# Seven of eleven gate and up chunk pairs of each feed-forward block computed with Strassen's seven half products

## The chip, the cores and the metric

The kernel runs on one core of a Trainium2 chip. The metric is the device time of one execution in microseconds (us). Five engines of the core take part: TensorE (PE: matrix products and transposes; its weight loads are listed as PEld), VectorE (DVE), ScalarE (ACT), GpSimd (POOL) and SyncE (SP), of which the last two here do little but issue DMA transfers. Each engine takes its instructions in the order of its own list, and waits where an operand or a buffer isn't ready.

## The reference

Two transformer blocks run one after the other over 256 tokens of width 2048, in float32. The first has differential attention beside a gated recurrence (hgrn2), cross attention to a memory of 256 tokens, and a feed-forward block. The second has a pooling mixer beside gated linear attention, and a feed-forward block. Both feed-forward blocks compute the same thing, and this is what the change touches:

```python
h = rms_norm(x, ffn_pre_g)                       # 256 x 2048
gate, up = jnp.split(h @ w_ffn_in, 2, axis=-1)   # each 256 x 5632
x = x + rms_norm((jax.nn.silu(gate) * up) @ w_ffn_out, ffn_post_g)
# second block: w_ffn_gate, w_ffn_up, w_ffn_down with the same shapes
```

## The kernel before

The 256 tokens are two tiles t of 128 rows. The activations of a tile stand in SBUF, the chip's working memory, in units of 128 x 512. A weight matrix is read in column chunks of 512; the hidden width of 5632 is eleven such chunks.

**Split weights.** `wsub` (L366 to L377) fetches a slab, 256 rows of a weight matrix by 512 columns, as one tile `raw` of 128x2x512 (written 128x1024 in the profile) by a 512 KB DMA that SP issues. ACT casts it to the matmul type fp32r (`wh`, L375), and DVE subtracts the cast from the raw slab (`wl`, L376). A float32 product is then made of three matmuls: high activation by high weight, high by low, low by high. There are `RAW_BUFS` = 4 buffers for raw slabs and `SPLIT_BUFS` = 8 pairs for `wh` and `wl`. Each slab therefore gives 2 (halves) x 2 (tiles) x 3 = 12 matmuls of 128x128 by 128x512.

**Activations** are transposed on PE (`transpose4`, L304) into PSUM, the memory of eight banks in which matmuls leave their results, and split in the same way into `hi` (ACT) and `lo` (DVE), L312 and L313. `normed` transposes x times the gain without the factor of the norm; the factor `rstd` is applied later, where a result is read from PSUM.

**Groups.** `group` runs the matmuls of one column chunk for both tiles (`mm_both`, L407), and hands each tile's PSUM bank to a consumer function. Small pieces of work that follow (transposes, norms) are generators; `spawn` puts one on a list and `tick` advances all of them once after each slab's matmuls. Instructions are written in program order, and a scheduler places them on the engines by priority: what stands under `ahead()` or `high_priority(offset)` is treated as if it had been written that much earlier, so that slabs are fetched and split before they are needed, as far as the buffers go.

**A feed-forward block** (`ffn`, L886) goes through the eleven chunks in three runs of 4, 4 and 3. In each run every chunk has a gate group and an up group, so 16 slabs and 192 matmuls; the gate's PSUM goes through Silu on ACT (L903, with scale `rstd`), and DVE multiplies it with the up result and `rstd` (`hh`, L908). The product is transposed and split. After a run come four groups of the down projection over its chunks. The sum y of the runs stays in SBUF: the first run writes y (L924), the second adds to it by a DMA that POOL issues (`y<-yp`, L929), the third adds on DVE (L931). The residual x stays in SBUF too.

**The boundary** ahead of a feed-forward block: the block before ends with a norm and the residual sum (`mg`, L490, four units to a tile), and `normed` takes each unit as it comes: transposes, `hi`, `lo`, and beside them the squares (`junk`, L299) and the factor (`v`, `y`, `t`, `r`, L286 to L295).

## Time and profile before

| what | value |
|---|---|
| median of 3 runs | 2867.75 us (2863.87 to 2867.84) |
| the profiled execution: its own time, its span | 2868.39 us, 2866.6 us |
| PE busy | 2837.1 us, 99% of the span |
| DVE busy | 1609.2 us, 56% |
| ACT busy | 1420.6 us, 50% |
| mean granted clock of TensorE | 0.998 of full speed |

The span is what the trace covers; 1.8 us of the execution's own time lie outside it. Matmuls overlap, so the mean duration of one in a table is longer than what it adds; what it adds is read from the chain that ended last, or from the distance between two starts. The same holds for DVE and ACT, where the next instruction can start shortly before the one ahead of it has ended. The profile's line numbers are those of the code above.

### The profile page before, as it was taken

To read this page: it belongs to the slowest core of one execution; us is meant where nothing else is said; L and a number is where in the kernel's file an instruction comes from. 1 tells how busy PE (TensorE), PEld (TensorE's weight loads), DVE (VectorE), ACT (ScalarE), POOL (GpSimd) and SP (SyncE) were. 2 spreads that over 40 slices of the span, in tenths; PEclk is the share of its full clock that TensorE was granted. 3 is DMA by queue.
4 is the path that set the end of the run, shared out by engine and by line. 5 is a ranking of instruction groups with operands and counts; after the bars stand their busy time and mean duration, and the time that the engine had idled before them with its cause. 6 is when DMAs were issued, how large, how long until landed. Compare 5 with 4: busy or idle time off the path is not lost.

```text
span 2866.6 us, 35074 instructions
## 1 busy us (share of the span) xinstructions
PE 2837.1 (99%) x13196; PEld 2351.5 (82%) x13196; DVE 1609.2 (56%) x2131; ACT 1420.6 (50%) x2116; POOL 58.8 (2%) x105
## 2 busy tenths in 40 slices
PE   8999999999999999999999999999999999999998
PEld 6788888778888888888888898888888888888887
DVE  6666586665444454456665566555565444554455
ACT  6554575664444444445655475444464444444443
POOL 1000000000000000000000000000000000000000
PEclk9999999999999999999999999999999999999999
DMA  7555546537656667765655557666747666667763
GB/s 238 163 176 168 180 156 203 169 124 215 192 190 195 187 190 214 201 201 186 201 154 166 159 152 215 196 194 191 230 138 230 189 191 194 187 191 214 202 202 124
DMA packets 277227, 535.14 MB, mean 187 GB/s; under 512 B 17769, under 2 KB 29669, under 8 KB 277056
## 3 DMA queue, kind: packets, MB, share of 16 engines
q1 hardware_dynamic: 269040, 512.70, 58.7%
q0 software_dynamic: 7440, 19.15, 2.7%
q8 instruction: 103, 1.69, 0.2%
q10 hardware_dynamic: 576, 1.05, 0.1%
q14 instruction: 68, 0.56, 0.1%
HBM read 522.86 MB, written 5.77 MB: 184 GB/s over the span
## 4 chain that ended last, share of the span: by engine, by line
PE 93%; ACT 3%; DMA 2%; DVE 2%; issue 1%; SPq 0%; DVEq 0%; ACTq 0%
PE mm L407 83%; PE tp L304 2%; PE lps L516 2%; PE mm L422 1%; PE mm L424 1%; PE mm L423 1%; DVE wl L376 1%; ACT hi L322 1%; ACT junk L299 1%; ACT wh L375 1%; DMA raw<-w_in 1%; PE po L581 0%; PE sc L686 0%; DMA raw<-w_ffn_gate 0%; DMA x<-x 0%
## 5 line engine op out<-in xcount | busy, mean ns | idle before, releaser
L376 DVE TENSOR_TENSOR wl<-raw,wh 128x1024 fp32r<-128x1024 f32 (+1 forms) x968 | 1175.6, 1215 | 1090.4 <-ACT wh L375 1088.2
L375 ACT CAST wh<-raw 128x1024 fp32r<-128x1024 f32 (+1 forms) x968 | 1011.9, 1047 | 1169.0 <-PE mm L407 1061.5
L407 PE MATMUL mm<-wh,hi 128*128 128x512 f32 (+1 forms) x3504 | 1091.9, 392 | 0.0
L407 PE MATMUL mm<-wl,hi 128*128 128x512 f32 (+1 forms) x3504 | 1079.8, 389 | 0.0
L407 PE MATMUL mm<-wh,lo 128*128 128x512 f32 (+1 forms) x3504 | 1077.8, 388 | 0.0
L407 PEld LDWEIGHTS mm<-wh,lo 128*128 128x128 f32 x3504 | 657.0, 188 | 133.7 <-issue 0.2
L407 PEld LDWEIGHTS mm<-wl,hi 128*128 128x128 f32 x3504 | 656.5, 188 | 132.2 <-issue 0.5
L407 PEld LDWEIGHTS mm<-wh,hi 128*128 128x128 f32 x3504 | 648.7, 188 | 130.0 <-issue 5.8
L422 PE MATMUL mm<-wh,hi 128*128 128x512 f32 (+1 forms) x304 | 121.0, 398 | 2.0 <-ACT hi L322 1.5
L423 PE MATMUL mm<-wl,hi 128*128 128x512 f32 (+1 forms) x304 | 119.7, 394 | 0.3 <-DVE wl L376 0.2
L424 PE MATMUL mm<-wh,lo 128*128 128x512 f32 (+1 forms) x304 | 119.9, 394 | 0.0
L322 ACT ACTIVATE hi<-tp,vec 128x128 fp32r<-128x128 f32 x224 | 71.7, 381 | 12.2 <-DVE lo L323 8.2
L323 DVE SCALAR_TENSOR_TENSOR lo<-tp,vec,hi 128x128 fp32r<-128x128 f32 x224 | 68.3, 344 | 14.7 <-ACT hi L322 14.2
L422 PEld LDWEIGHTS mm<-wh,hi 128*128 128x128 f32 x304 | 57.6, 190 | 17.3 <-ACT hi L322 7.3
L424 PEld LDWEIGHTS mm<-wh,lo 128*128 128x128 f32 x304 | 57.5, 189 | 13.0 <-DVE lo L323 2.3
L423 PEld LDWEIGHTS mm<-wl,hi 128*128 128x128 f32 x304 | 57.7, 190 | 11.2 <-DVE wl L376 1.5
L516 PEld LDWEIGHTS lps<-qd,kd 128*128 128x128 f32 x448 | 58.3, 191 | 4.2 <-issue 0.3
L516 PE MATMUL lps<-qd,kd 128*128 128x64 f32 x448 | 56.2, 268 | 0.0
L333 ACT ACTIVATE tok<-mm,r 128x512 f32<-128x512 f32 x44 | 30.1, 690 | 33.6 <-PE mm L407 33.6
L903 ACT ACTIVATE sg<-mm,r 128x512 f32<-128x512 f32 x44 | 30.4, 690 | 28.8 <-PE mm L407 28.8
L312 ACT CAST hi<-tp 128x512 fp32r<-128x512 f32 x54 | 29.7, 589 | 20.5 <-PE tp L304 20.3
L929 POOL DMA_DIRECT2D y<-yp x16 | 13.9, 872 | 1214.1 <-ACT yp L928 1214.1
(243 smaller groups left out, 1220.1 us busy)
## 6 DMA issues: line engine op xcount, KB each, us to landing
raw<-w_in SPq DMA_DIRECT2D x256, 512.0 KB, 3.7
raw<-w_ffn_in SPq DMA_DIRECT2D x176, 512.0 KB, 3.8
raw<-w_ffn_out SPq DMA_DIRECT2D x88, 512.0 KB, 3.6
raw<-w_ffn_gate SPq DMA_DIRECT2D x88, 512.0 KB, 4.1
raw<-w_ffn_up SPq DMA_DIRECT2D x88, 512.0 KB, 3.9
raw<-w_ffn_down SPq DMA_DIRECT2D x88, 512.0 KB, 4.3
raw<-w_out SPq DMA_DIRECT2D x64, 512.0 KB, 4.3
raw<-w_branch_b SPq DMA_DIRECT2D x32, 512.0 KB, 3.7
```

The costliest lines, as they stand in the source:

```text
L304: self.nc.tensor.transpose(ps[:, i, :], src[:, i * P:(i + 1) * P], self.ident)
L322: nc.scalar.activation(hi[:, i, :], ps[:, i, :], AF.Copy, scale=g)
L323: nc.vector.scalar_tensor_tensor(lo[:, i, :], ps[:, i, :], g, hi[:, i, :].bitcast(F32), ALU.mult, ALU.subtract)
L333: self.nc.scalar.activation(dst, ps, AF.Copy, scale=scale)
L375: nc.scalar.copy(hi[:, :, :ncol], raw[:, :, :ncol])
L376: nc.vector.tensor_tensor(lo[:, :, :ncol], raw[:, :, :ncol], hi[:, :, :ncol].bitcast(F32), ALU.subtract)
L407: nc.tensor.matmul(ps[t][:, :ncol], hT[t][kk // 4][p][:, kk % 4, :], w[:, i, :ncol], start=kk == first and p == 0 and w is wh, stop=kk == ...
L422: nc.tensor.matmul(ps[:, :ncol], xh, wh[:, i, :ncol], start=kk == first, stop=False)
L423: nc.tensor.matmul(ps[:, :ncol], xh, wl[:, i, :ncol], start=False, stop=False)
L424: nc.tensor.matmul(ps[:, :ncol], xl, wh[:, i, :ncol], start=False, stop=kk == last)
L516: nc.tensor.matmul(ps[:, h, :], lhs[:, i, :], rhs[:, i, :], start=c == 0, stop=c == cph - 1)
L903: nc.scalar.activation(u, ps, AF.Silu, scale=rstd[t])
```

## The change

It concerns the gate and up products alone. With A the 256 x 2048 activations as a 2 x 2 grid (tile t by half of the 2048) and B the 2 x 2 grid of a weight column pair (half of the 2048 by gate or up), the four blocks of A @ B are eight half products. In seven of the eleven chunk pairs (1, 2, 4, 5, 7, 8, 10) the function `seven` computes them as seven products of sums, by Strassen's scheme in Winograd's form, instead. The other four pairs (0, 3, 6, 9) run as before (`plain`).

- `seven` has four steps s. A step fetches four slabs (upper and lower half of the rows, of gate and of up), forms four sums of slabs in place on DVE (L490, L493, L495, L500), and splits seven weight parts (cast L386, subtraction L387), named P1, Q3, Q5, Q7, P2, Q6, Q4. Each part has 6 matmuls (L506 to L508, 2 halves x 3), 42 to a step and 168 to a chunk pair, into seven PSUM banks. At the end one ACT copy (L512) and seven DVE sums (L513 to L519) make the four blocks; then Silu and a multiplication for each tile.
- `combos` makes the sums of activations once for each feed-forward block: 24 DVE operations and 8 ACT casts of 128x512, as a job that begins behind chunk 0.
- The activations must now be scaled ahead of the sums. `normed(scaled=True)` computes the four squares and the factor first, then makes four scaled copies (ACT), and transposes these.
- x goes to DRAM ahead of the block (`spilled`), and the partial y stays in DRAM; both are read again in the last run of down groups, x by SP and y by POOL. The chunks, fast ones marked by True, and the down runs are ordered by `FF_ORDER`, with four down runs in place of three.
- `ACT_UNITS` goes from 54 to 51 and `RAW_BUFS` from 4 to 6, in the whole program.

```diff
-ACT_UNITS = 54
-RAW_BUFS = 4
+ACT_UNITS = 51
+RAW_BUFS = 6
 SPLIT_BUFS = 8
...
+SLAB_AHEAD = 70
+POST_AHEAD = 150
+
+FF_ORDER = ((0, False), (1, True), (0, 2), (2, True), (3, False), (4, True), (2, 5),
+            (5, True), (6, False), (7, True), (5, 8), (8, True), (9, False), (10, True), (8, 11))
...
+    def combos(self, hT):
...
+        a = {(t, k): [hT[t][2 * k + j] for j in range(2)] for t in range(NT) for k in range(2)}
+        S = {"P1": a[0, 0], "P2": a[0, 1], "Q4": a[1, 1], "Q5": [None] * 2, "Q6": [None] * 2, "Q7": [None] * 2, "Q3": [None] * 2}
+
+        def split(v):
+            hi, lo = self.uT("sh"), self.uT("sl")
+            nc.scalar.copy(hi, v)
+            nc.vector.tensor_tensor(lo, v, hi.bitcast(F32), ALU.subtract)
+            return hi, lo
...
+        def job():
+            for j in range(2):
+                v21, v22 = full(1, 0, j), full(1, 1, j)
+                yield 2
+                nc.vector.tensor_tensor(v22, v21, v22, ALU.subtract)
+                S["Q5"][j] = split(v22)
+                yield 2
...
+    def seven(self, Wa, Wb, c0, S, consume):
...
+        for s in range(4):
+            with self.tc.high_priority(offset=max(0, min(SLAB_AHEAD, self.tc.cur_priority - self.base))):
+                w = {}
+                x = self.slab(Wa, 2 * s, c0)
+                w["P1"] = self.parts(x)
+                b12 = self.slab(Wb, 2 * s, c0)
+                nc.vector.tensor_tensor(x, x, b12, ALU.add)
+                b22 = self.slab(Wb, 8 + 2 * s, c0)
+                w["Q3"] = self.parts(b22)
+                nc.vector.tensor_tensor(b12, b12, b22, ALU.add)
+                w["Q5"] = self.parts(x)
+                nc.vector.tensor_tensor(x, x, b22, ALU.add)
+                w["Q7"] = self.parts(b12)
+                b21 = self.slab(Wa, 8 + 2 * s, c0)
+                w["P2"] = self.parts(b21)
+                w["Q6"] = self.parts(x)
+                nc.vector.tensor_tensor(x, x, b21, ALU.add)
+                w["Q4"] = self.parts(x)
+            for n, (wh, wl) in w.items():
+                for i in range(2):
+                    kk = 2 * s + i
+                    xh, xl = (v[:, kk % 4, :] for v in S[n][kk // 4])
+                    nc.tensor.matmul(bank[n], xh, wh[:, i, :], start=kk == 0, stop=False)
+                    nc.tensor.matmul(bank[n], xh, wl[:, i, :], start=False, stop=False)
+                    nc.tensor.matmul(bank[n], xl, wh[:, i, :], start=False, stop=kk == 7)
+                self.tick()
+        with self.tc.high_priority(offset=POST_AHEAD):
+            p1, c11, e, c12 = (self.unit(name=n) for n in ("p1", "c11", "e", "c12"))
+            nc.scalar.copy(p1, bank["P1"])
+            nc.vector.tensor_tensor(c11, bank["P2"], p1, ALU.add)
+            nc.vector.tensor_tensor(p1, bank["Q6"], p1, ALU.subtract)
...
+            if scaled:
+                acc, xs = self.small(4, "acc"), []
+                for j, u in enumerate(start(t)):
+                    self.square_sum(u, acc[:, j:j + 1])
+                    xs.append(u)
...
+                r = self.rsqrt_mean(s, D)
+                for j in range(4):
+                    u = self.unit(name="xn")
+                    self.scaled_copy(u, xs[j], r)
+                    xs[j] = u
...
-                        u = self.unit(name="hh")
-                        nc.vector.scalar_tensor_tensor(u, ps, rstd[t], sg[t], ALU.mult, ALU.mult)
...
+            for a, b in FF_ORDER:
+                if b is True:
+                    fast(a)
+                elif b is False:
+                    plain(a)
+                    if S is None:
+                        S, more = self.combos(hT)
+                        self.spawn(more)
+                else:
+                    down(a, b)
```

How the instructions stand on the engines, in three places. A row gives the line, the operation, and output <- inputs by the program's names with their numbers.

On DVE before, in the first feed-forward block where one chunk pair of a run follows another, the list is one subtraction for each slab, with the two `hh` and the two `lo` of the chunk pair in between:

```order
L376 TENSOR_TENSOR wl_1429_6630<-raw_1427_6627,wh_1428_6629 128x1024
L376 TENSOR_TENSOR wl_1432_6636<-raw_1430_6633,wh_1431_6635 128x1024
L908 SCALAR_TENSOR_TENSOR hh_1410_6593<-mm_1408_6495,r_1203_5548,sg_1382_6443 128x512
L908 SCALAR_TENSOR_TENSOR hh_1411_6595<-mm_1409_6496,r_1256_5750,sg_1383_6445 128x512
L376 TENSOR_TENSOR wl_1435_6642<-raw_1433_6639,wh_1434_6641 128x1024
L313 TENSOR_TENSOR lo_1441_6670<-tp_1438_6653,hi_1440_6669 128x512
L313 TENSOR_TENSOR lo_1443_6674<-tp_1439_6658,hi_1442_6673 128x512
L376 TENSOR_TENSOR wl_1448_6768<-raw_1446_6765,wh_1447_6767 128x1024
```

Each of these `wl` has 12 matmuls to serve.

On DVE after, the third step of chunk 2 (which follows a down run); `raw_1530`, `raw_1533`, `raw_1534` and `raw_1541` are its four slabs:

```order
L387 TENSOR_TENSOR wl_1532_6931<-raw_1530_6928,wh_1531_6930 128x1024
L387 TENSOR_TENSOR wl_1536_6940<-raw_1534_6937,wh_1535_6939 128x1024
L490 TENSOR_TENSOR raw_1530_6928<-raw_1530_6928,raw_1533_6934 128x1024
L493 TENSOR_TENSOR raw_1533_6934<-raw_1533_6934,raw_1534_6937 128x1024
L387 TENSOR_TENSOR wl_1538_6945<-raw_1530_6928,wh_1537_6944 128x1024
L387 TENSOR_TENSOR wl_1540_6950<-raw_1533_6934,wh_1539_6949 128x1024
L495 TENSOR_TENSOR raw_1530_6928<-raw_1530_6928,raw_1534_6937 128x1024
L387 TENSOR_TENSOR wl_1543_6956<-raw_1541_6953,wh_1542_6955 128x1024
L387 TENSOR_TENSOR wl_1545_6960<-raw_1530_6928,wh_1544_6959 128x1024
L500 TENSOR_TENSOR raw_1530_6928<-raw_1530_6928,raw_1541_6953 128x1024
L387 TENSOR_TENSOR wl_1547_6965<-raw_1530_6928,wh_1546_6964 128x1024
```

Seven subtractions and four sums of the same size now serve 42 matmuls. The sum L493 stands right behind L490, whose result the next `wl` needs; L500 and the last `wl` (Q4's) stand next to each other, and between them ACT has to cast the sum that L500 has just written.

At the end of the same chunk's fourth step two of the seven sums over PSUM (`c11`, `p1`) stand between those two:

```order
L387 TENSOR_TENSOR wl_1563_7042<-raw_1548_7010,wh_1562_7041 128x1024
L500 TENSOR_TENSOR raw_1548_7010<-raw_1548_7010,raw_1559_7035 128x1024
L513 TENSOR_TENSOR c11_1567_7093<-mm7_1491_6761,p1_1566_7092 128x512
L514 TENSOR_TENSOR p1_1566_7092<-mm7_1492_6762,p1_1566_7092 128x512
L387 TENSOR_TENSOR wl_1565_7047<-raw_1548_7010,wh_1564_7046 128x1024
L515 TENSOR_TENSOR e_1568_7094<-mm_1489_6759,p1_1566_7092 128x512
L387 TENSOR_TENSOR wl_1572_7111<-raw_1570_7108,wh_1571_7110 128x1024
```

The last subtraction of the chunk, `wl_1565`, comes behind them, and the sums go on between the splits of the next chunk.

On PE before, each weight slab meets both tiles (`hi_1187`, `hi_1244`):

```order
L407 MATMUL mm_1672_7881<-wh_1655_7847,hi_1187_5471 128x512
L407 MATMUL mm_1673_7882<-wh_1655_7847,hi_1244_5681 128x512
L407 MATMUL mm_1672_7881<-wl_1656_7848,hi_1187_5471 128x512
L407 MATMUL mm_1673_7882<-wl_1656_7848,hi_1244_5681 128x512
L407 MATMUL mm_1672_7881<-wh_1655_7847,lo_1188_5472 128x512
L407 MATMUL mm_1673_7882<-wh_1655_7847,lo_1245_5682 128x512
```

On PE after, one part, Q3 of chunk 2's first step, meets one sum of activations (`sh_1320` and `sl_1321`, from `combos`):

```order
L506 MATMUL mm_1488_6758<-wh_1499_6775,sh_1320_6036 128x512
L507 MATMUL mm_1488_6758<-wl_1500_6776,sh_1320_6036 128x512
L508 MATMUL mm_1488_6758<-wh_1499_6775,sl_1321_6037 128x512
L506 MATMUL mm_1488_6758<-wh_1499_6775,sh_1320_6036 128x512
L507 MATMUL mm_1488_6758<-wl_1500_6776,sh_1320_6036 128x512
L508 MATMUL mm_1488_6758<-wh_1499_6775,sl_1321_6037 128x512
```

PE's list goes from 12013 rows to 11677: 336 fewer, 24 for each of the 14 fast chunk pairs.

## Rows read from the trace of the kernel before

**Rows 1.** The page, part 1: busy time, share, instructions of each engine.

```profile
PE 2837.1 (99%) x13196; PEld 2351.5 (82%) x13196; DVE 1609.2 (56%) x2131; ACT 1420.6 (50%) x2116; POOL 58.8 (2%) x105
```

**Rows 2.** Windows over most of each feed-forward block: stretch, length, busy (instructions), clock, DMA.

```profile
640.00:1330.00 690.00, 690.00 (x3089) 571.84 (x3088) 344.30 (x308) 303.30 (x322) 9.19 (x12) 1.00 0.66 199
2172.00:2820.00 648.00, 647.90 (x2902) 536.89 (x2901) 318.16 (x284) 281.85 (x298) 9.15 (x12) 1.00 0.67 196
```

**Rows 3.** The chain that ended last, from 664 us: start, length, what.

```profile
664.07 43.57 PE mm L407 x192
707.64 0.87 PE tp L304 x8
708.52 43.54 PE mm L407 x192
```

**Rows 4.** Groups by form on DVE and ACT: busy us, mean ns, idle before.

```profile
L376 DVE TENSOR_TENSOR wl<-raw,wh 128x1024 fp32r<-128x1024 f32 x928 | 1134.9, 1224 | 1061.7 <-ACT wh L375 1059.5
...
L535 DVE TENSOR_TENSOR e<-b 128x512 f32<-128x512 f32 x56 | 38.2, 682 | 0.0
L313 DVE TENSOR_TENSOR lo<-tp,hi 128x512 fp32r<-128x512 f32 x54 | 34.8, 685 | 2.8 <-ACT hi L312 0.7
...
L908 DVE SCALAR_TENSOR_TENSOR hh<-mm,r,sg 128x512 f32<-128x512 f32 x44 | 31.0, 746 | 3.7 <-PE mm L407 3.7
...
L375 ACT CAST wh<-raw 128x1024 fp32r<-128x1024 f32 x928 | 976.7, 1054 | 1145.1 <-PE mm L407 1044.8 <-issue 45.4 <-DMA raw<-w_in 10.9
...
L928 ACT COPY yp<-mm 128x512 f32<-128x512 f32 x16 | 9.4, 587 | 11.5 <-PE mm L407 11.5
```

**Rows 5.** DVE's timeline, four pieces: start, length, instruction, idle before it.

```profile
2146.91 4.63 DVE L376 TENSOR_TENSOR wl<-raw,wh 128x1024 fp32r<-128x1024 f32 x4 [0.33 <-ACT wh L375]
...
2174.98 1.28 DVE L313 TENSOR_TENSOR lo<-tp,hi 128x512 fp32r<-128x512 f32 x2
2177.14 1.23 DVE L376 TENSOR_TENSOR wl<-raw,wh 128x1024 fp32r<-128x1024 f32 x1 [0.89 <-ACT wh L375]
2179.87 1.23 DVE L376 TENSOR_TENSOR wl<-raw,wh 128x1024 fp32r<-128x1024 f32 x1 [1.50 <-ACT wh L375]
```

**Rows 6.** The timeline of ACT and DVE: a cast and the split behind it.

```profile
2101.57 1.04 ACT L375 CAST wh<-raw 128x1024 fp32r<-128x1024 f32 x1
...
2102.64 1.23 DVE L376 TENSOR_TENSOR wl<-raw,wh 128x1024 fp32r<-128x1024 f32 x1 [0.25 <-ACT wh L375]
```

**Rows 7.** DVE's timeline at the boundary ahead of the first feed-forward block.

```profile
622.69 0.15 DVE L487 TENSOR_REDUCE pssq<-acc 128x1 f32<-128x4 f32 x1
...
623.73 0.16 DVE L292 TENSOR_TENSOR t<-t,v 128x1 f32<-128x1 f32 x1
623.92 0.15 DVE L293 TENSOR_SCALAR t<-t 128x1 f32<-128x1 f32 x1
...
624.31 2.74 DVE L490 SCALAR_TENSOR_TENSOR mg<-mg,r,mg 128x512 f32<-128x512 f32 x4
```

**Rows 8.** ACT's timeline at the same boundary.

```profile
625.09 0.63 ACT L299 ACTIVATE junk<-mg 128x512 f32<-128x512 f32 x1 [1.59 <-DVE mg L490]
...
631.10 1.28 ACT L903 ACT_TABLE_LOAD   x1
...
633.87 1.28 ACT L289 ACT_TABLE_LOAD   x1
```

**Rows 9.** PE's timeline at the start of the program.

```profile
25.34 1.08 PE L304 MATMUL tp<-ident,x 128*128 128x128 f32 x4 [3.08 <-DMA x<-x]
```

**Rows 10.** Windows at the start and at the boundary, columns as in rows 2.

```profile
20.00:25.30 5.30, 2.27 (x10) 1.36 (x8) 3.93 (x9) 3.23 (x7) 0.19 (x1) 1.00 0.92 281
25.34:29.20 3.86, 3.86 (x16) 3.38 (x17) 2.46 (x7) 3.61 (x10) 3.69 (x8) 0.56 1.01 371
592.00:642.00 50.00, 48.35 (x222) 38.15 (x221) 35.84 (x84) 37.23 (x90) 0.00 (x0) 1.00 0.33 103
```

**Rows 11.** The page, part 6: a slab's DMA, KB, us from issue to landing.

```profile
raw<-w_ffn_gate SPq DMA_DIRECT2D x88, 512.0 KB, 4.1
```

More of the change, by code (lines that the diff above doesn't have):

```diff
@@ L438, in load_x, with normed @@
         return xs
-    def normed(self, start, pre):
+    def normed(self, start, pre, scaled=False):
         rstd, hT = [None] * NT, [[None] * 4 for _ in range(NT)]
@@ L456, in job @@
                 yield 1
+            if scaled:
+                rstd[t] = r
+                return
             acc = self.small(4, "acc")
@@ L491, in add_normed, with spilled, f, boundary @@
             yield mg[j]
-    def boundary(self, start, pre):
+    def spilled(self, done, xd):
+        def f(t):
+            for j, u in enumerate(done(t)):
+                self.nc.gpsimd.dma_start(xd[t * P:(t + 1) * P, j * CW:(j + 1) * CW], u)
+                yield u
+        return f
+    def boundary(self, start, pre, scaled=False):
         xs = [None] * NT
@@ L501, in first @@
                 yield u
-        rstd, hT, job = self.normed(first, pre)
+        rstd, hT, job = self.normed(first, pre, scaled)
         return xs, rstd, hT, job
@@ L894, in run @@
         def run(job):
-            for bi, (b0, nb) in enumerate(blocks):
-                hid = [[None] * nb for _ in range(NT)]
-                last = bi == len(blocks) - 1
-                for c in range(nb):
-                    sg = [None] * NT
-                    def g_in(t, ps):
-                        u = self.unit(name="sg")
-                        nc.scalar.activation(u, ps, AF.Silu, scale=rstd[t])
-                        sg[t] = u
-                    def u_in(t, ps, c=c, sg=sg):
-                        u = self.unit(name="hh")
-                        nc.vector.scalar_tensor_tensor(u, ps, rstd[t], sg[t], ALU.mult, ALU.mult)
-                        def put(pair):
-                            hid[t][c] = pair
-                        yield from self.to_T(u, put)
-                    self.group(Wg, (b0 + c) * CW, hT, ks, g_in, apart=bi == 0 and c == 0)
-                    self.group(Wu, (b0 + c) * CW, hT, ks, u_in)
+            hid, S = [[None] * n_all for _ in range(NT)], None
@@ new lines, in put, with f, plain, g_in @@
+            def put(t, c):
+                def f(pair):
+                    hid[t][c] = pair
+                return f
+            def plain(c):
+                sg = [None] * NT
+                def g_in(t, ps):
+                    sg[t] = self.unit(name="sg")
+                    nc.scalar.activation(sg[t], ps, AF.Silu)
+                def u_in(t, ps):
+                    u = self.unit(name="hh")
+                    nc.vector.tensor_tensor(u, ps, sg[t], ALU.mult)
+                    yield from self.to_T(u, put(t, c))
+                self.group(Wg, c * CW, hT, ks, g_in, apart=c == 0)
+                self.group(Wu, c * CW, hT, ks, u_in)
@@ new lines, in fast, with all_in @@
+            def fast(c):
+                def all_in(*cs):
+                    with self.tc.high_priority(offset=POST_AHEAD):
+                        for t in range(NT):
+                            g, u = cs[2 * t:2 * t + 2]
+                            nc.scalar.activation(g, g, AF.Silu)
+                            nc.vector.tensor_tensor(u, u, g, ALU.mult)
+                    for t in range(NT):
+                        self.spawn(self.to_T(cs[2 * t + 1], put(t, c)))
+                self.seven(Wg, Wu, c * CW, S, all_in)
@@ L915, in run, with down @@
+            def down(b0, b1):
+                last = b1 == n_all
                 if last:
                     self.ln_exp_set()
+                    for t in range(NT):
+                        for n in range(4):
+                            y[t][n] = self.unit(name="y")
+                            nc.gpsimd.dma_start(y[t][n], yd[t][n])
+                    for t, row in enumerate(self.load_x(xd)):
+                        x[t][:] = row
                 for n in range(4):
```

96 lines of the change are left out of this document (64 added, 32 removed).

## The prediction

> **What bounds the kernel now.** I read the page's part 1 first: PE is busy for 99% of the span and DVE for 56% [rows 1]. Then the windows over the two feed-forward blocks, because an average says nothing of one stage: in 690 us and in 648 us PE has no idle time to speak of, at the full granted clock, while DVE works about half of each, 344.3 and 318.2 us [rows 2]. Then the chain of waits from 664 us: 192 matmuls in 43.57 us, so 0.2269 us for one, 0.87 us of transposes, and 44.45 us from one chunk pair to the next [rows 3]. So these stages are bound by PE; fewer matmuls make them shorter for as long as every other engine keeps up.
>
> The engine to ask about is DVE. A weight subtraction of 128x1024 lasts 1.224 us [rows 4], but four back to back take 4.63 us: (4.63 - 1.22) / 3 = 1.14 us from start to start. In a chunk pair they start 2.73 us apart and wait for the cast [rows 5], which itself had waited for PE to free a buffer [rows 4]. So DVE uses 1.14 of every 2.73 us there.
>
> **The matmuls.** 24 fewer in each of 14 fast chunk pairs are 336 x 0.2269 = 76.2 us, if PE stays the bound: 2868.4 - 76.2 = 2792 us, counted as all sums here from the profiled execution's own 2868.39 us, which lies 0.6 us over the median.
>
> **One step of a fast chunk.** PE needs 42 x 0.2269 = 9.53 us. DVE has seven subtractions and four sums, all of 128x1024. The sum of slabs has no row. The nearest is L535, which takes two float32 operands from SBUF and writes float32: 682 ns for 512 elements, where the subtraction of 512 takes 685 [rows 4] and starts 0.60 us after the one before [rows 5]. So I price a sum like a subtraction: 11 x 1.14 = 12.54 us. On top of that come waits inside the step. L490's result goes through L493 to the next `wl`, and a sum right behind its input starts 0.04 us after that has ended (small dependent operations: 623.73 + 0.16 to 623.92) [rows 7], not 0.08 us before: 0.1 us at each of two places. The long wait is behind L500: its result has to be written (1.22), cast on ACT (1.05) [rows 4], and the split starts 0.03 us behind the cast (2101.57 + 1.04 to 2102.64) [rows 6]. The split thus starts 1.22 + 0.04 + 1.05 + 0.03 = 2.34 us after L500, instead of 1.14: 1.2 us. Everything behind it on DVE, the next step's splits, waits too. A step is 12.54 + 0.2 + 1.2 = 13.9 us on DVE against 9.53 on PE: inside a fast chunk DVE is the bound.
>
> **How much of that is hidden.** DVE can run ahead only as far as there are `wh`/`wl` pairs: eight. When the work before a fast chunk ends, seven hold the parts of its step 0, and the eighth still holds the last slab of that work. So step 0 is hidden (13.9 us, out of 16 x 1.59 us of free DVE in a plain chunk pair), and the other three are not. From the end T of the work before: the eighth pair comes free, and behind a down run ACT first copies `yp` (0.59) [rows 4] and then casts (1.05): T + 1.6. Steps 1 and 2: 27.8. Step 3 up to L500: nine operations and its two small waits, 10.5; L500 1.14; the two sums over PSUM that stand there, 2 x 0.62, which cover the cast; the last split 1.22; the last five matmuls, which wait for it, 1.13: 15.2. Together 44.6 us, then 0.2 to the next group and 0.88 of transposes of its own: 45.7 against 44.45, +1.25. Behind a plain pair there is no `yp` (-0.35), the two `lo` of that pair are done inside the fast chunk (+1.2), and its transposes fall into PE's waits (-0.88): the same to 0.1. So 24 matmuls, 5.4 us, are saved, and nothing is left: 14 x 1.25 = +18 us. The slabs' DMAs are no part of this: a slab lands in 4.1 us [rows 11], and 16 slabs in 45.7 us are the rate of before (share 0.66) [rows 2].
>
> **Activation sums.** 24 operations of 128x512 fall on DVE in the first fast chunk, where DVE is the bound: 24 x 0.60 [rows 5] = 14.4, plus about 1 for waits on their own casts, less one 1.2 us wait behind L500 that they fill: +14.3 in each block, +29.
>
> **The boundaries.** Before, the transposes of a tile could start with its first residual unit. Now all four (2.74 from the start of the first, 0.7 of it needed before too) [rows 7], the last square (0.63) [rows 8], the factor (622.69 to 624.31, 1.6) [rows 7] and a scaled copy (no row; the ACT copy of `yp`, 0.59 [rows 4]) come first: 2.0 + 0.6 + 1.6 + 0.6 + 0.2 of hand-overs = 5.0. Two table loads of 1.28 us on ACT between factor and Silu [rows 8] have no reason left. PE hardly idles there now, 1.65 of 50 us [rows 10]: other work covers a part of the wait and may cover more or less of the longer one, so 0 to 10 each; I take 5: +10.
>
> **The start.** PE waits 3.08 us for the second tile of x [rows 9], whose transfers stand on SP behind seven slabs that need raw buffers; with six of these they go out earlier. But the DMA engines are already at a share of 0.92 there [rows 10]: 0 to -5, I take -3.
>
> **At nothing:** spills and reloads of x and y. POOL and SP issue them, partial y has a whole run of chunks to land in, and the reloads stand before the last down groups. If that cover is gone, it is a few us at the end of each block.
>
> Sum: 18 + 29 + 10 - 3 = +54: 2868.4 + 54 = 2922 us, 1.9% slower.
>
> **Bounds.** From below: no waits inside a step (12.54; a fast chunk 45.7 - 2 x 1.4 - 0.2 = 42.7, -1.75 x 14 = -25), sums of activations partly in idle time (+20), boundaries 0, start -5: 2858. From above: each operation on DVE starts only 0.03 us after the one before has ended (1.25; a step 11 x 1.25 + 1.1 = 14.9, a fast chunk about 48.8, +4.35 x 14 = +61), activation sums 24 x 0.75 (+36), boundaries +20, start 0: 2985.
>
> **Rivals.**
> (a) Faster. The mechanism is the step's time on DVE: at break-even 14d = -(29 + 10 - 3), d = -2.6, so a fast chunk takes 41.9 and, with three steps of it in sight, a step about 12.6 with the wait behind L500 still in it: the point is 1.2 us less in each step. If a sum of slabs cost half (0.57), a step were 4 x 0.57 = 2.3 shorter, a fast chunk 6.8, and the total 2922 - 14 x 6.8 = 2827. For it: no row shows a sum of this size. Against it: L535, and the eight pairs. Chance 0.11 of faster, 0.06 of landing within 0.2% of before.
> (b) The dearer step. If operations start only when the one before has ended (1.22), a step takes 14.6, a fast chunk 2.3 more, and the activation sums 2 more for each block: 2922 + 32 + 4 = 2958. Against it: 4.63 us for four [rows 5]; for it: in a fast chunk most have a dependent one close behind. Chance 0.15. The Trainium skill, "VectorE: DVE Perf Modes", section "The DRAIN you can't avoid", says that the next operation doesn't start until the pipeline is empty. By that rule 2958 would be the forecast; the four subtractions at 1.14 us that last 1.22 disagree with it by 0.08 us each, and the trace decides.
> (c) The clock. In the row before PE's wait of 3.08 us PE was busy for 2.27 of 5.30 us at a granted clock of 1.00, behind it the clock was 0.56 for 3.86 us [rows 9, 10]. In a fast step PE is busy for 9.5 of 13.9 us, with its longest wait between Q3 and Q5, about 2.0 us. If the clock stayed at its lower level, 1.2 GHz, a step would be 42 x 0.4538 = 19.1 us on PE, above DVE's 13.9, and a fast chunk 4 x 19.1 + 1.8 = 78 us, 32 longer: 2922 + 14 x 32 = 3370. Chance 0.04. The Trainium skill, "TensorE: Matmul & The Clock Gate", section "A second HAM failure mode: psum-queue depth-cycling", tells of a kernel whose short idle times between groups of matmuls made the clock go back and forth. By that rule some part of these 450 us would be lost; of the rows here only a wait of 3.08 us was followed by a lower clock.
> (d) PE stays the bound and the whole 76 us come: 2792. DVE's 11 operations against 9.53 us exclude it unless both prices are far off: 0.02, inside the 0.11.
>
> **How the numbers follow.** The forecast (2880 to 2945) has 0.64, (b) and what lies above it up to 2990 0.15, (c) 0.04, within 0.2% 0.06, faster 0.11. The measurement can't tell less than about 0.2%, 5.7 us, from no change. Slower is 0.64 + 0.15 + 0.04 = 0.83. The range goes from 2860, which takes in the no-change case and a little of (a), to 2990.
>
> **What would show it.** PE's matmuls fall by 336, DVE's busy time rises by 168 + 224 operations of 1.22 and 98 + 48 of 0.69 to about 2190 us. The chain in a fast chunk goes through `wl` and the sums on DVE, with PE waiting 6 to 7 us in it; fast chunks take 45 to 46 us, the first of each block about 60; Q4's split waits for its cast 1.2 us in three steps of four. The boundaries show squares, factor and scaled copies in the chain. I am wrong if PE has no waits on `wl` there, if sums of slabs start less than 1.1 us apart, if steps after the first are hidden too, or if the granted clock falls below 1.00 throughout the fast chunks.

## The result and the profile after

The changed kernel takes 2953.35 us (median of 4 runs, 2952.43 to 2955.13), the kernel before 2867.11: a ratio of 1.0304, 95% interval 1.0286 to 1.0322. It is slower, as forecast, by 86 us where 54 had been forecast.

The page of the changed kernel, part 1, beside [rows 1]:

```profile
PE 2811.8 (95%) x12860; PEld 2287.3 (77%) x12860; DVE 2132.8 (72%) x2669; ACT 1602.5 (54%) x2342; POOL 98.7 (3%) x169
```

336 matmuls fewer, but PE's share falls from 99 to 95%, and DVE's rises from 56 to 72%: 523 us more, where the prediction had about 580.

Where the time went is read from the start of the same matmuls in both traces. Up to the first block's gate group, and through the whole second mixer, PE does the same work in the same order; the distance between the two traces changes at these places only:

| stage | forecast, us | measured, us |
|---|---|---|
| start of the program | -3 | -4.1 |
| cross attention | 0 | -4.7 |
| the two boundaries | +10 | +8.7 and +9.3 |
| the first fast pair of each block | +14.3 + 1.25 each | +15.8 and +16.5 |
| the twelve other fast pairs | +15 | +30.8 |
| plain pairs and down runs between them | 0 | +12.9 |
| sum (the spans differ by 85.2; the forecast's terms were rounded up to 54) | +53 | +85.2 |

The forecast's 15 us count with each fast pair its own eight transposes (0.87 us). Behind a down run PE makes those of a pair only in the group that follows, so six of the twelve pairs are measured without them; counted as in the forecast, the two rows are +36 and +7.7.

Windows of the changed kernel (columns as in [rows 2]): PE's wait at the first boundary and the stretch behind it, the same in the first fast pair, then the second fast pair as a whole:

```profile
600.00:606.00 6.00, 1.84 (x9) 1.18 (x7) 5.93 (x8) 5.90 (x14) 0.84 (x2) 1.00 1.00 342
606.10:613.00 6.90, 4.30 (x18) 4.14 (x19) 3.68 (x14) 5.87 (x20) 0.00 (x0) 0.51 0.85 307
671.00:678.00 7.00, 3.43 (x8) 2.41 (x9) 7.00 (x10) 2.51 (x4) 0.00 (x0) 0.51 0.00 0
768.00:814.00 46.00, 40.49 (x170) 31.05 (x168) 42.29 (x39) 25.54 (x28) 1.08 (x2) 1.00 0.53 160
```

In the fast pair DVE is busy for 42.29 of 46 us and PE for 40.49, where before both rows of [rows 2] had PE at 100%. Two stretches have a granted clock of about half, the lower of the two levels; both begin inside a long wait of PE and go on behind it, as its timeline shows (start, length, instruction, idle before it and what ended that):

```profile
608.70 3.68 PE L309 MATMUL tp<-ident,xn 128*128 128x128 f32 x16 [6.86 <-ACT xn L338]
...
674.57 0.80 PE L506 MATMUL mm<-wh,sh 128*128 128x512 f32 x1 [7.43 <-ACT sh L449]
```

One step of the second fast pair on DVE, from Q4's split of one step to that of the next (rows as in [rows 5]; L387 is a split, the other lines are the four sums):

```profile
782.43 3.50 DVE L387 TENSOR_TENSOR wl<-raw,wh 128x1024 fp32r<-128x1024 f32 x3 [1.19 <-ACT wh L386]
785.85 1.22 DVE L490 TENSOR_TENSOR raw<-raw,raw 128x1024 f32<-128x1024 f32 x1
787.10 1.23 DVE L493 TENSOR_TENSOR raw<-raw,raw 128x1024 f32<-128x1024 f32 x1
788.26 2.48 DVE L387 TENSOR_TENSOR wl<-raw,wh 128x1024 fp32r<-128x1024 f32 x2
790.66 1.22 DVE L495 TENSOR_TENSOR raw<-raw,raw 128x1024 f32<-128x1024 f32 x1
791.80 2.50 DVE L387 TENSOR_TENSOR wl<-raw,wh 128x1024 fp32r<-128x1024 f32 x2
794.33 1.22 DVE L500 TENSOR_TENSOR raw<-raw,raw 128x1024 f32<-128x1024 f32 x1
796.74 1.22 DVE L387 TENSOR_TENSOR wl<-raw,wh 128x1024 fp32r<-128x1024 f32 x1 [1.19 <-ACT wh L386]
```

It takes 796.74 - 782.43 = 14.31 us, and the wait behind L500 is there as worked out: 1.19 us for Q4's cast. Back to back the splits start 1.14 us apart, and the sums start 1.14 to 1.25 us before what follows: a sum costs what a split costs. The other gaps are L490 to L493, 1.25 (L493 overwrites a slab that L490 still reads), the second split of each pair, 1.26 and 1.28, and Q6's split to L500, 1.25. The two pairs were not in the forecast: Q7's and Q6's splits need casts of sums too, and from the start of a sum over ACT's cast to its split it is 2.4 us here (794.33 to 796.74), while two operations on DVE fill only 2.28.

PE's side of the same chunk: all its waits are on ACT's casts and DVE's splits, 0.4 to 1.0 us long, and the first of the eight ends at 793.07. Up to there PE lives on DVE's lead.

```profile
793.07 0.50 PE L507 MATMUL mm<-wl,hi 128*128 128x512 f32 x1 [0.49 <-DVE wl L387]
...
796.76 0.51 PE L506 MATMUL mm<-wh,hi 128*128 128x512 f32 x1 [0.87 <-ACT wh L386]
797.71 0.50 PE L506 MATMUL mm<-wh,hi 128*128 128x512 f32 x1 [0.44 <-ACT wh L386]
...
802.56 0.50 PE L506 MATMUL mm<-wh,sh 128*128 128x512 f32 x1 [0.61 <-ACT wh L386]
803.82 0.50 PE L506 MATMUL mm<-wh,sh 128*128 128x512 f32 x1 [0.76 <-ACT wh L386]
```

### The profile page after: what moved, and what is told of

It reads as the page before. It is cut to its first block, busy times and chain, and to the rows that moved or that the text cites. A ratio compares the mean times of both kernels' runs of the same rounds, so it can differ in the third digit from the quotient of the medians.

```text
span 2951.8 us, 35680 instructions
## 1 busy us (share of the span) xinstructions
PE 2811.8 (95%) x12860; PEld 2287.3 (77%) x12860; DVE 2132.8 (72%) x2669; ACT 1602.5 (54%) x2342; POOL 98.7 (3%) x169
## 5 line engine op out<-in xcount | busy, mean ns | idle before, releaser
L387 DVE TENSOR_TENSOR wl<-raw,wh 128x1024 fp32r<-128x1024 f32 (+1 forms) x1136 | 1364.4, 1215 | 631.4 <-ACT wh L386 623.3
L386 ACT CAST wh<-raw 128x1024 fp32r<-128x1024 f32 (+1 forms) x1136 | 1170.6, 1046 | 1046.5 <-PE mm L418 580.5
L418 PE MATMUL mm<-wh,hi 128*128 128x512 f32 (+2 forms) x2608 | 827.2, 394 | 13.6 <-ACT wh L386 13.5
L418 PE MATMUL mm<-wl,hi 128*128 128x512 f32 (+2 forms) x2608 | 807.1, 389 | 0.9 <-DVE wl L387 0.9
L418 PE MATMUL mm<-wh,lo 128*128 128x512 f32 (+2 forms) x2608 | 803.5, 388 | 0.0
L418 PEld LDWEIGHTS mm<-wh,lo 128*128 128x128 f32 x2608 | 489.3, 188 | 98.9 <-issue 0.2
L418 PEld LDWEIGHTS mm<-wl,hi 128*128 128x128 f32 x2608 | 488.4, 188 | 99.4 <-DVE wl L387 3.6
L506 PE MATMUL mm<-wh,sh 128*128 128x512 f32 x448 | 182.3, 407 | 48.1 <-ACT wh L386 30.4
L508 PE MATMUL mm<-wh,sl 128*128 128x512 f32 x448 | 175.9, 393 | 0.7 <-DVE sl L450 0.7
L506 PE MATMUL mm<-wh,hi 128*128 128x512 f32 x336 | 137.2, 408 | 30.4 <-ACT wh L386 30.4
L506 PEld LDWEIGHTS mm<-wh,sh 128*128 128x128 f32 x448 | 84.5, 189 | 85.2 <-ACT wh L386 50.0
L508 PE MATMUL mm<-wh,lo 128*128 128x512 f32 x336 | 132.7, 395 | 0.0
L433 PE MATMUL mm<-wh,hi 128*128 128x512 f32 (+1 forms) x304 | 121.4, 399 | 4.3 <-ACT hi L327 4.2
L435 PE MATMUL mm<-wh,lo 128*128 128x512 f32 (+1 forms) x304 | 119.2, 392 | 0.0
L434 PE MATMUL mm<-wl,hi 128*128 128x512 f32 (+1 forms) x304 | 119.2, 392 | 0.0
L506 PEld LDWEIGHTS mm<-wh,hi 128*128 128x128 f32 x336 | 63.8, 190 | 59.0 <-ACT wh L386 46.8
L508 PEld LDWEIGHTS mm<-wh,sl 128*128 128x128 f32 x448 | 84.6, 189 | 20.3 <-DVE sl L450 2.8
```

The lines of the kernel that those rows point to most:

```text
L386: nc.scalar.copy(hi[:, :, :ncol], raw[:, :, :ncol])
L387: nc.vector.tensor_tensor(lo[:, :, :ncol], raw[:, :, :ncol], hi[:, :, :ncol].bitcast(F32), ALU.subtract)
L418: nc.tensor.matmul(ps[t][:, :ncol], hT[t][kk // 4][p][:, kk % 4, :], w[:, i, :ncol], start=kk == first and p == 0 and w is wh, stop=kk == ...
L433: nc.tensor.matmul(ps[:, :ncol], xh, wh[:, i, :ncol], start=kk == first, stop=False)
L434: nc.tensor.matmul(ps[:, :ncol], xh, wl[:, i, :ncol], start=False, stop=False)
L435: nc.tensor.matmul(ps[:, :ncol], xl, wh[:, i, :ncol], start=False, stop=kk == last)
```

## The experiments

All times below are medians; the ratio is to runs of the kernel before on the same chip.

**raw6: the kernel before with the buffers of the change.**

```diff
-ACT_UNITS = 54
-RAW_BUFS = 4
+ACT_UNITS = 51
+RAW_BUFS = 6
```

> The kernel before with RAW_BUFS 6 and ACT_UNITS 51 alone. In the changed kernel's trace the matmuls run 4.1 us ahead of before from the start on, and 8.8 us ahead from the cross attention on. Theory: both come from the two more raw buffers: 2867 - 9 = 2858 us. Rival: the second gain comes from what else the change moved (priorities, fewer units held); then 2863 us, and 2867 if the start too has another cause.

2858.17 us, ratio 0.9973 (0.9963 to 0.9984). PE's wait for x at the start, 3.08 us at the longest [rows 9], is down to 1.2:

```profile
PE tp L304 <- DMA x<-x: 2.2, 3, 1.2
```

The theory holds for both gains: the two constants by themselves are worth 8 us (they weren't tried apart), and this part of the change is the only one that pays. In the cross attention PE had waited 2.10 us for a copy on ACT, up to 553.01 us of the trace before, and from 554.4 to 558.0 the granted clock there was 0.53; neither is left.

**scaled: the scaled norm alone, in the kernel before.**

```diff
-            xs = list(start(t))
+            acc, xs = self.small(4, "acc"), []
+            for j, u in enumerate(start(t)):
+                self.square_sum(u, acc[:, j:j + 1])
...
+                self.scaled_copy(u, xs[j], r)
...
-                        nc.scalar.activation(u, ps, AF.Silu, scale=rstd[t])
+                        nc.scalar.activation(u, ps, AF.Silu)
```

> The kernel before with the scaled norm alone ahead of both feed-forward blocks (squares, factor and scaled copies ahead of the transposes; Silu and hh without the factor); x and y stay in SBUF. In the changed kernel the boundaries take 8.7 and 9.3 us longer where 5 each had been forecast. Theory: all of it is the longer way to the first transpose, with the lower clock that follows PE's wait: 2867 + 18 = 2885 us, with PE at a granted clock of 0.5 for some 7 us behind each boundary. Rival: the forecast's 5 us each is the way itself, and the rest comes from the spill of x by POOL or from the first fast chunk's slabs: 2877 us.

2885.72 us, ratio 1.0070 (1.0056 to 1.0084): 19.9 us more, so the boundary's 18 us need neither the spill nor the fast pairs. The window in which PE's wait of 8.53 us for the first scaled copy ends (at 615.58):

```profile
612.10:618.90 6.80, 3.32 (x16) 3.32 (x17) 3.83 (x12) 6.23 (x17) 0.00 (x0) 0.50 0.56 182
```

Why the way is 11 us for the first tile and not 5 stands in ACT's timeline of the changed kernel: casts of weights stand between the squares, in its fixed order, and the first square itself starts 1.35 us after its input, which DVE began at 597.40.

```profile
598.75 0.63 ACT L304 ACTIVATE junk<-mg 128x512 f32<-128x512 f32 x1
...
599.38 1.03 ACT L386 CAST wh<-raw 128x1024 fp32r<-128x1024 f32 x1
600.31 0.63 ACT L304 ACTIVATE junk<-mg 128x512 f32<-128x512 f32 x1
...
600.93 1.04 ACT L386 CAST wh<-raw 128x1024 fp32r<-128x1024 f32 x1
...
603.43 0.63 ACT L304 ACTIVATE junk<-mg 128x512 f32<-128x512 f32 x1
...
607.92 2.56 ACT L338 ACTIVATE xn<-mg,r 128x512 f32<-128x512 f32 x4 [0.80 <-DVE r L300]
```

Four squares take from 598.75 to 604.15, where four in a row would take 2.9 (0.72 apart); the factor takes from there to 607.92, 3.8 us in place of 1.6, since on ACT three squares of the other tile stand ahead of its logarithm (606.21) and a fourth ahead of its exponential (606.93). The scaled copies begin at 607.92 and the transposes at 608.70, 11.3 us after the first residual unit. The second tile, with no casts between, takes 617.79 to 624.00, 6.2 us.

**q4early and q4first: the wait behind the fourth sum.** In q4early the fourth sum goes to P2's slab and is written ahead of Q6's parts:

```diff
                 w["P2"] = self.parts(b21)
-                w["Q6"] = self.parts(x)
-                nc.vector.tensor_tensor(x, x, b21, ALU.add)
-                w["Q4"] = self.parts(x)
+                nc.vector.tensor_tensor(b21, x, b21, ALU.add)
+                w["Q6"] = self.parts(x)
+                w["Q4"] = self.parts(b21)
```

> The changed kernel with the fourth sum written into the slab of P2, ahead of Q6's split instead of behind it, so that Q6's split stands between that sum and Q4's split. Theory: DVE's chain sets the step, and 1.2 us of its 14.3 are the wait for Q4's cast; a step takes 13.1 to 13.2 us, a fast chunk 2.3 us less (two of its three exposed steps, the third has two sums there already), 14 x 2.3 = 32: 2953 - 32 = 2921 us. Rival: the eight pairs of split weights set the pace, and DVE would wait for PE instead: within 5 us of 2953.

2948.11 us, ratio 1.0283 (1.0267 to 1.0298), within the rival's 5 us. But the edit had not reached the engine: the scheduler put Q6's split ahead of the sum (L499 here) again, and the same wait stands behind it.

```profile
777.87 2.50 DVE L387 TENSOR_TENSOR wl<-raw,wh 128x1024 fp32r<-128x1024 f32 x2
780.29 1.22 DVE L499 TENSOR_TENSOR raw<-raw,raw 128x1024 f32<-128x1024 f32 x1
782.70 1.23 DVE L387 TENSOR_TENSOR wl<-raw,wh 128x1024 fp32r<-128x1024 f32 x1 [1.19 <-ACT wh L386]
```

So this run says nothing on the theory. In q4first P2's slab is fetched and split earlier, so that the sum can follow the third one:

```diff
+                b21 = self.slab(Wa, 8 + 2 * s, c0)
+                w["P2"] = self.parts(b21)
                 nc.vector.tensor_tensor(x, x, b22, ALU.add)
+                nc.vector.tensor_tensor(b21, x, b21, ALU.add)
                 w["Q7"] = self.parts(b12)
-                b21 = self.slab(Wa, 8 + 2 * s, c0)
-                w["P2"] = self.parts(b21)
                 w["Q6"] = self.parts(x)
-                nc.vector.tensor_tensor(x, x, b21, ALU.add)
-                w["Q4"] = self.parts(x)
+                w["Q4"] = self.parts(b21)
```

> The changed kernel with P2's slab fetched and split before the third sum, and the fourth sum written into that slab right behind the third, so that on DVE one or two splits stand between the fourth sum and Q4's split (in q4early the scheduler had put Q6's split ahead of the sum again, and the wait of 1.19 us in each step was still there). Theory, as before: the wait for Q4's cast is 1.2 us of a step of 14.3; a step takes 13.1 to 13.2 us, a fast chunk 2.4 us less, 14 x 2.4 = 34: 2953 - 34 = 2919 us. Rival: the eight pairs and PE's pace hold DVE, the wait goes elsewhere: within 6 us of 2953.

2902.49 us, ratio 1.0126 (1.0110 to 1.0141): 51 us less, where 34 had been expected; the rival is out. The step, from L490 to L490:

```profile
783.66 1.22 DVE L490 TENSOR_TENSOR raw<-raw,raw 128x1024 f32<-128x1024 f32 x1
784.91 1.23 DVE L493 TENSOR_TENSOR raw<-raw,raw 128x1024 f32<-128x1024 f32 x1
786.08 2.36 DVE L387 TENSOR_TENSOR wl<-raw,wh 128x1024 fp32r<-128x1024 f32 x2
788.35 1.22 DVE L497 TENSOR_TENSOR raw<-raw,raw 128x1024 f32<-128x1024 f32 x1
789.49 1.22 DVE L387 TENSOR_TENSOR wl<-raw,wh 128x1024 fp32r<-128x1024 f32 x1
790.62 1.22 DVE L498 TENSOR_TENSOR raw<-raw,raw 128x1024 f32<-128x1024 f32 x1
791.76 4.78 DVE L387 TENSOR_TENSOR wl<-raw,wh 128x1024 fp32r<-128x1024 f32 x4
796.45 1.22 DVE L490 TENSOR_TENSOR raw<-raw,raw 128x1024 f32<-128x1024 f32 x1
```

796.45 - 783.66 = 12.79 us, 1.52 less than before: the wait for Q4's cast is gone, and with it the small ones at Q7 and Q6, and no idle time is left on DVE. 12.54 had been worked out for a step without waits. Three exposed steps of 1.4 to 1.5 us are the 4.2 us by which a fast pair falls (46.25 to 42.0).

**nosums: no sums of slabs.** Each of the four lines with `tensor_tensor(..., ALU.add)` over slabs is left out.

> The changed kernel without the four sums of slabs in each step (the parts are made of the slabs as they were fetched, so the products are others); all splits, matmuls and sums over PSUM stay. Theory: DVE has seven operations left, 8.0 us, and PE's 9.53 us a step is the bound again: a fast chunk takes 38.1 + 0.9 of transposes + about 1 of hand-over = 40 us instead of 46.3 or 47.4, and the first of a block 12 less: 2953 - 12 x 6.8 - 2 x 12 = 2847 us, faster than before. Rival: what is slow is the chain of slab, cast and split with its buffers, not DVE's load: then a fast chunk falls by less than 3 us and the time stays above 2905.

2824.19 us, ratio 0.9853 (0.9838 to 0.9868). The second fast pair, from first to last matmul:

```profile
755.30:793.40 38.10, 38.10 (x169) 31.54 (x168) 33.15 (x28) 30.87 (x32) 1.08 (x2) 1.00 0.73 235
```

38.10 us, and 168 x 0.2269 is 38.1: PE is the bound again, without a gap. The time is 23 us below the expectation, mostly because a pair falls by 8.2 to 8.4 us and not by 6.8. So the splits, casts, slabs and buffers are fast enough; what turns the gain into a loss are the four sums on DVE.

**poolsums: the sums on POOL.**

```diff
-                nc.vector.tensor_tensor(x, x, b12, ALU.add)
+                nc.gpsimd.tensor_tensor(x, x, b12, ALU.add)
...
```

> The changed kernel with the four sums of slabs of each step on POOL instead of DVE. No row shows such a sum on POOL. Theory: DVE's eleven operations a step are what makes fast chunks as long as plain ones; with seven left (8.0 us) PE's 9.53 is the bound again if POOL makes a sum in less than some 2.2 us: fast chunks of 40 to 42 us and about 2953 - 14 x 5.5 = 2876 us. If POOL takes twice as long as DVE or more (over 2.5 us), its four sums and the casts between them are the new chain of a step, 13 us and more, and the time stays near 2950 or rises. Rival to the theory: latency from sum to cast to split is what counts, not DVE's load; then the time does not fall even where POOL needs less than 2 us.

3180.29 us, ratio 1.1096 (1.1081 to 1.1112). The groups on POOL, and DVE's splits in the same run (columns as in [rows 4]):

```profile
L495 POOL TENSOR_TENSOR raw<-raw,raw 128x1024 f32<-128x1024 f32 x56 | 187.8, 3354 | 73.3 <-DVE wl L387 73.3
...
L500 POOL TENSOR_TENSOR raw<-raw,raw 128x1024 f32<-128x1024 f32 x56 | 134.6, 2403 | 159.1 <-DVE wl L387 152.6 <-DMA raw<-w_ffn_in 3.3 <-DMA raw<-w_ffn_up 3.2
```

```profile
L387 DVE TENSOR_TENSOR wl<-raw,wh 128x1024 fp32r<-128x1024 f32 x1096 | 1523.1, 1404 | 864.9 <-ACT wh L386 857.9 <-DMA raw<-w_out 1.5
```

A sum takes 2.4 to 3.4 us on POOL, so the second case holds; a fast pair takes about 60 us. DVE's splits rise from 1.224 to 1.404 us on average, and the average mixes two kinds: the 210 that overlap a sum on POOL take 2.18 us, the longest 3.69, and the 886 others 1.22. Four splits back to back, 4.63 us before [rows 5], can take 8.26:

```profile
810.88 8.26 DVE L387 TENSOR_TENSOR wl<-raw,wh 128x1024 fp32r<-128x1024 f32 x4 [3.35 <-ACT wh L386]
```

The Trainium skill, "GPSIMD Engine Reference", section "Key points", says that POOL shares its way to SBUF with DVE instructions that have two SBUF inputs, and that DVE is about twice as fast for such work; both agree with these rows.

**nocombos: no sums of activations.** The seven products take blocks of the activations as they are.

```diff
...
+                S["Q5"][j], S["Q7"][j], S["Q6"][j], S["Q3"][j] = a[1, 0][j], a[1, 1][j], a[0, 0][j], a[0, 1][j]
...
```

> The changed kernel without the sums of activations (the seven products take blocks of the activations instead, so the results are others): 24 operations on DVE and 8 casts fewer in each block. Theory: these cost DVE's time one for one in the first fast chunk, which takes 60.2 us where others behind a plain pair take 47.4: 13 us less for each block, and no lower clock there: 2953 - 27 = 2926 us. Rival: that chunk is long because it is the first behind the boundary, with buffers empty; then it stays near 60 and the time within 6 us of 2953.

2932.55 us, ratio 1.0231 (1.0215 to 1.0246). The first fast pair goes from 60.2 us to 47.9, like the others behind a plain pair; in the second block from 61.0 to 47.7. That is 12.3 and 13.3 us for the theory's 13 each; of these 26 us, 21 reach the total.

**split9: nine pairs.**

```diff
-ACT_UNITS = 51
+ACT_UNITS = 47
...
-SPLIT_BUFS = 8
+SPLIT_BUFS = 9
```

> The changed kernel with nine pairs of split weights instead of eight, and 47 activation units instead of 51, which pay for it. Theory: DVE's lead at the start of a fast chunk is as many parts as there are pairs beside the one still in use; one more is a seventh of a step, 14.3 / 7 = 2.0 us, for each fast chunk, 14 x 2 = 28: 2925 us. Rival 1: slabs (six raw buffers) or casts limit the lead: no change within 5 us. Rival 2: four units fewer make transposes or outputs wait: above 2958 us.

2921.36 us, ratio 1.0192 (1.0175 to 1.0209): 32 us less. Most fast pairs fall by 2.6 to 3.0 us (46.3 to 43.2, 47.4 to 44.8), while the stretch between the blocks' fast pairs gets 6 us longer. The lead is set by the pairs of buffers: with one more DVE gets further ahead, and neither rival came.

**sixfast: the order of chunks.**

```diff
-FF_ORDER = ((0, False), (1, True), (0, 2), (2, True), (3, False), (4, True), (2, 5),
-            (5, True), (6, False), (7, True), (5, 8), (8, True), (9, False), (10, True), (8, 11))
+FF_ORDER = ((0, False), (1, False), (2, True), (0, 3), (3, True), (4, False), (5, True), (3, 6),
+            (6, True), (7, False), (8, True), (6, 9), (9, True), (10, False), (9, 11))
```

> The changed kernel with another order of chunks: two plain pairs ahead of the first fast one, six fast pairs in each block instead of seven and three down runs of three chunks and one of two. Theory: the sums of activations cost their time only because they stand in a fast chunk, where DVE is the bound (without them that chunk fell from 60.2 to 47.9 us); in a plain pair DVE has 1.59 of every 2.73 us free, and they are hidden there. The first fast chunk takes 47 to 48 us as the others behind a plain pair do, 12.5 us less in each block, and one fast pair in each block turns plain, 2 to 3 us less: 2953 - 30 = 2923 us. Rival: the sums come late or hold up the splits of the plain pair, and move the wait there: 2940 us or more.

2926.89 us, ratio 1.0213 (1.0196 to 1.0230), as expected: the first fast pair takes 47.5 us, like the others behind a plain pair (47.4).

**best9, best8, best9r5: all of it together.** best9 is q4first with sixfast's order, nine pairs and 47 units; best8 has eight pairs and 51 units instead, best9r5 nine pairs, 49 units and five raw buffers.

> All that shortened the changed kernel in one: the fourth sum early (as in q4first), nine pairs of split weights with 47 units (as in split9), and the order of chunks of sixfast. By addition from the changed kernel's 2953: -51, -32 x 12 / 14 and -30 give 2845 us, below the kernel before with six raw buffers (2858). Rival: once a step takes 12.8 us and starts two parts ahead, PE's 9.53 and the hand-over between chunks bind, the gains overlap, and it stays at 2855 to 2875; in every case the boundaries' 20 us remain.

> best9 with the changed kernel's eight pairs and 51 units. In best9 the fast chunks took what had been expected (37.4 to 41.2 us from first to last matmul, against 43.3 and 44.4), but the stretch from the end of the first feed-forward block's fast chunks to the second's took 1024 us against 972 in sixfast, with PE idle in the second block's mixer. Theory: 47 units are too few there and that alone ate 52 us; with 51 units the gains add: sixfast's 2927 - 51 x 12 / 14 = 2883 us, and the stretch is back at 972. Rival: the early fourth sum or the order of chunks disturbs the mixer; then the stretch stays above 1000 and the time near 2905.

> best9 with five raw buffers and 49 units in place of six and 47. Theory: two units more give back at least half of what the mixer lost, and five raw buffers are enough for the fast chunks: 2904 - 26 to 52, so 2852 to 2878 us; at its lower end that is below the kernel before with six raw buffers (2858). Rival: 49 units are still too few (2890 or more), or the fifth slab is missed in fast chunks, where a step holds four at once: these then take 2 us more each, over 2880.

best9 2904.29 us, ratio 1.0135 (1.0120 to 1.0151), neither of what had been expected; best8 2876.08, 1.0037 (1.0025 to 1.0049); best9r5 2909.81, 1.0151 (1.0138 to 1.0164). The stretch between the fast pairs of the two blocks (the last down run, the second mixer, two plain pairs), best9 first, then best8:

```profile
1235.75:2259.74 1023.99, 973.71 (x4528) 818.16 (x4529) 594.90 (x830) 585.04 (x834) 16.71 (x31) 0.98 0.59 181
```

```profile
1253.54:2223.98 970.44, 959.44 (x4531) 805.67 (x4530) 595.17 (x830) 508.56 (x776) 16.72 (x31) 1.00 0.62 191
```

1024 against 970 us for the same work of PE. What differs is ACT: 834 instructions against 776, 76 us more busy time. The 58 more are table loads, 1.28 us each; they stand in ACT's list ahead of a function that the load before did not cover. The kernel asks for one (L151, `ln_exp_set`) that serves logarithm (L367, L293) and exponential (L368, L294) alike. In best8 it stands behind the block's last Silu (L1026):

```profile
1277.75 0.60 ACT L1026 ACTIVATE sg<-mm 128x512 f32<-128x512 f32 x1
1278.37 1.28 ACT L151 ACT_TABLE_LOAD   x1
```

In best9 the scheduler put it ahead of that Silu, for which another load follows at once, and from there to the next L151 each change between logarithm and exponential has a load of its own:

```profile
1260.79 1.28 ACT L151 ACT_TABLE_LOAD   x1
1262.08 1.28 ACT L1026 ACT_TABLE_LOAD   x1
1263.37 1.09 ACT L1026 ACTIVATE sg<-mm 128x512 f32<-128x512 f32 x2
...
1655.00 1.28 ACT L367 ACT_TABLE_LOAD   x1
1656.29 0.63 ACT L367 ACTIVATE sg<-sd 128x512 f32<-128x512 f32 x1
...
1657.34 1.28 ACT L368 ACT_TABLE_LOAD   x1
```

In the mixer these loads stand on the way to `sg`, for which PE's transposes wait:

```profile
PE tp L309 <- DVE sg L1115: 17.6, 8, 5.9
```

The whole program has 7 table loads in the changed kernel, sixfast and best8. It has 16 in split9, where an L151 stands ahead of a Sigmoid (L1211), late in this stretch (6 us longer), and 70 in best9 and best9r5 (1024 and 1027 us). So what the traces show to stretch the mixer is an order on ACT; best8 has the early sum and the order of chunks too, without it. Whether the ninth pair or the fewer units moved the load in the list was not tried apart, nor was a run made with the load held in its place. In best9r5 the rival's first case came about (2890 or more); its fast pairs take 38.9 to 42.0 us. (Where the expectation of best8 has 43.3 and 44.4 us for fast pairs of the changed kernel, it counts them about 3 us shorter than they are counted here.) best8's 2876 us is 7 below its expectation. No version that keeps the four sums, and so the result, gets below raw6's 2858 us: best8 still carries the boundaries' 20 us and fast pairs of 42 to 43 us.

## Why the prediction was right, point by point

The mechanism was the one forecast, and the sizes came out low: 2953 us lies above 2880 to 2945, which had been given 0.64, in the stretch up to 2990 that had been given to (b).

- **DVE as the bound of a fast pair: right, and shown.** Without the four sums a fast pair takes PE's 38.1 us (nosums); with them DVE is busy for 42.29 of 46.
- **A sum priced like a split from L535's row: right.** 1.14 to 1.25 us from start to start.
- **The wait behind L500: right,** 1.19 us measured for 1.2 worked out, and shown by taking it away (q4first).
- **A step of 13.9 us: right in kind, too small by 0.4.** Measured 14.31. The missing part are Q7's and Q6's splits, each 0.12 to 0.14 us behind a cast that starts when a sum has ended, and 0.07 more at Q4. The two places of 0.1 us were four, and at L493 it is not L490's result that is waited for but the slab that L490 reads. Three exposed steps of twelve fast pairs make 15 of the 29 us that the forecast lacked in fast, plain and down groups. Fast pairs behind a plain one and behind a down run are alike, as forecast: 47.4 us, and 46.3 with 0.87 for the pair's own transposes, which there come later, so 47.1. With the lower clock in two of them, worth about 2 us, and some 4 us that stay open, the twelve pairs account for 21. The rest, about 8, falls on the down runs and plain pairs, most of it on some that follow a fast pair (the first down run of the first block takes 46.2 us for 44.4 of matmuls and transposes, with a wait of 0.89 us for a split); they start with DVE having little lead, and I had them at nothing.
- **Eight pairs as the lead: right,** and one more pair is worth 2.6 to 3.0 us instead of a seventh of a step (split9).
- **The sums of activations: right.** +15.8 and +16.5 for the first pair, 15.5 forecast; nocombos and sixfast show where they come from.
- **The boundaries, 5 us each: the term that was most off for its size.** Measured 8.7 and 9.3. Its chain was right, but I summed only its links; on ACT the squares stood behind casts that the scheduler had put between them, so that the first tile's way took 11.3 us, and the clock was at its lower level for 6.8 us from inside PE's wait on. The two causes were not tried apart; as PE was busy for 4.30 of the 6.90 us at half, the clock can have cost about 2 us (an estimate) and the way the rest.
- **The start, -3: right in place,** -4.1, and another -4.7 in the cross attention that I did not see.
- **The rivals.** (b), operations that start only when the one before has ended, fell: three splits back to back take 3.50 us, so 1.14 us apart, in the fast pairs too. The time of 2953 us lies close to (b)'s 2958, but for other reasons. (c) came about in a small part: in ten of the fourteen fast pairs the clock was granted in full throughout, as in that from 768 to 814 us; in the first of each block it was lower from inside a wait of 7.4 us on; and at the end of one of these and of two others it was at about half for 3.4 us, behind waits of no more than 1 us. PE's short waits come only in the last 21 us of a pair, and not in every step as (c) had it:

```profile
1111.30:1114.70 3.40, 3.40 (x10) 2.62 (x9) 3.40 (x5) 3.40 (x5) 0.00 (x0) 0.50 0.61 191
2278.60:2282.00 3.40, 3.40 (x10) 2.66 (x9) 3.40 (x5) 3.24 (x4) 0.00 (x0) 0.51 0.64 184
2462.90:2466.30 3.40, 3.27 (x8) 2.59 (x9) 3.40 (x6) 3.40 (x5) 0.00 (x0) 0.51 0.68 224
```

The chunk that ends at the first of these takes 48.25 us, others behind a plain pair 47.4: about a microsecond each. The rule of the Trainium skill, "TensorE: Matmul & The Clock Gate", section "A second HAM failure mode: psum-queue depth-cycling", that short idle times can do this, agrees with these rows, and the price is some 3 us, not 450. (a) put its break-even at a step of about 12.6 us; q4first comes to 12.79 and, with the boundaries dearer than forecast, is still 1.3% slower. (d) would have needed sums that cost next to nothing: nosums shows that its mechanism, PE as the bound, was 4 x 1.14 us a step away.

## What to carry to other kernels

Fewer matmuls pay only where the engine that prepares their operands has room: count its operations for each matmul saved, at their distance from start to start, and ask how many of them the buffers let it do ahead. A result that goes from one engine over a second one back to the first costs its whole way (2.4 us here for a sum, a cast and a hand-over) unless that much other work stands between; in a list that a scheduler writes, look at the list, since a moved line of code may not move the instruction. When a change has several parts, time the side effects alone: here two constants, the smallest of its edits, are worth 8 us by themselves. And when a buffer count changes, count the table loads too: they follow the order of ACT's list, and 63 more of them undid what the ninth pair gave.

## What the runs showed of the hardware

- From inside waits of PE of 6.9 us (the boundary), 7.4 us (the first fast pair) and 8.5 us (scaled) on, the granted clock was about 0.5 for 6.8 to 10.2 us; waits of 0.4 to 1.0 us in the last 21 us of a fast pair mostly left it at 1.00, but three times 3.4 us at half followed such waits.
- A 128x1024 float32 sum took 2.4 to 3.4 us on POOL against 1.22 on DVE; DVE splits that overlapped one took 2.18 us on average, the others 1.22.
- A table load on ACT took 1.28 us; 70 of them in place of 7 came with a mixer stretch of 1024 us in place of 970.
